# One layer of a hybrid decoder on one core: a block of weights multiplied in two products instead of three in three parts of the program

## The chip, the core and the metric

The kernel runs on one core of a Trainium2 chip. The metric is the device time of one execution in microseconds; three executions of the kernel before took 1103.18, 1103.72 and 1104.4 us, with a median of 1103.72 us.

## What is computed

The input x has 256 tokens of 2048 features, in float32, and there is one layer. The reference, cut to what matters:

```python
h = rmsnorm(x, attn_norm_g)
z = h @ w_in                                    # pool | q | k | v | indexer
y_pool = pool_mixer(u_pool, pool_w, pool_scale) # 4 groups, windows 2, 4, 8, 16
y_attn = dsa_attention(q, k, v, q_idx, k_idx, w_idx)
x = x + jnp.concatenate([y_pool, y_attn], axis=-1) @ w_out
up = rmsnorm(x, ffn_norm_g) @ w_up              # then a causal convolution of width 3
out = x + (silu(gate) * val) @ w_down
```

## The kernel before

**Exact splits.** Every float32 weight is split on the chip into a high part `whi` (ScalarE, L103) and a low part `wlo` (VectorE, L104), and so is every activation: `xhl` is the normalized x, `yhl` the mixers' output, `ghl` the gated feed-forward activation, each with a high and a low part of 256 tokens beside each other. A product of a weight block (128 x 128) and 256 tokens is the sum of three: high weight by high tokens, high weight by low tokens, low weight by high tokens.

**Two ways to form it with features on partitions.** `mm_feat` (L209 to 212) multiplies the high weight by both token parts in one instruction of 512 columns (L211), whose second 256 columns go to the second half of the PSUM bank, and the low weight by the high tokens in one of 256 columns (L212). Whoever reads the result must add the two halves. `mm_feat1` (L214 to 218) makes three products of 256 columns (L216, L217, L218) that all add up in the first half, so that there is nothing to add at the end. Each product loads its weight block first, so L216 and L217 load the same one twice. Before the change `mm_feat` serves w_up and the first 14 of the 16 output tiles of w_down; `mm_feat1` serves the pool columns of w_in (`pool_chunk`, L231), w_out (`mm_o`, L266), the last two tiles of w_down (t = 14 and 15, L316) and the small mixing matrices of the pool groups (`pool_mix`, L571). The other columns of w_in are formed with tokens on partitions (`mm_tok`, L205 to 207, products of 320 to 512 columns).

**Pieces.** The weights arrive as a stream of 384 pieces of up to 1024 columns (8 blocks each for the parts above). At step i the main loop asks for a load, splits piece i+2 (`prep`), calls the side work listed for step i (the `at(...)` table) and issues the products of piece i. `whi` and `wlo` have four buffers each. A scheduler then sets the final order on each engine.

**Accumulators.** `Acc` takes a [128, 2, 512] buffer, of which there are two, or for the last two w_down tiles a single bank. Readers are `pool_u` (L519, one multiplication by the norm, L522), `x1_out` (L580, adds the residual, L583, then splits the new x and sums its squares), `up_out` (L610), `down_out` (L636) and `down_out1` (L643, adds the residual and stores one tile, L646 and L647).

**The pool chain.** For each of four groups n: pool_u, then pool_win (sliding sums L533, difference L537, edges L540 and L542, split into `dhl` L544 and L545), then pool_mix (products `pm`, results into `yhl`, L573 and L574), all as side work between the pieces. The last group's columns are the last of w_in, and w_out follows directly; its first pair of tiles is ordered so that the rows of the last group come last.

Of the kernel before, what the change touches and what calls it, by code (L numbers as in the profile page):

```python
# [15 lines left out]
P = 128  # L16
# [11 lines left out]

# columns of the packed parameters
C_AG, C_FG, C_PS, C_QG, C_KG, C_IC, C_CW, C_CB = 0, 16, 32, 40, 41, 42, 58, 58 + 3 * 2 * NF  # L30
C_N = C_CB + 2 * NF

# the indexer's columns: heads (with the key and the head weights in the first chunk)
IHEADS = (5, 6, 5)
IWIDTH = (5 * 64 + 80, 6 * 64, 5 * 64)
# pool groups, the widest window first
GROUPS = (3, 2, 1, 0)
# the columns of w_in: indexer, keys, queries, values, pool groups
ORDER = ("i0", "i1", "i2", "k0", "k1", "u0", "q0", "q1", "u1", "v0", "u2", "v1", "u3")
# [4 lines left out]
def hybrid_kernel(ctx, tc, xT, par, wI0, wI1, wI2, wA, wU, wP, wO, wUp, wDn, out):  # L44
# [12 lines left out]

# [1 line left out]
    warm = cp.tile([P, 512], BF16, name="warm")  # L59
# [8 lines left out]
    nc.gpsimd.memset(ones, 1.0)  # L68
    # loads the table of functions
    tab = cp.tile([P, 1], F32, name="tab")  # L70
# [3 lines left out]

# [1 line left out]
    class Unit:  # L76
        """Columns of weights that are loaded together."""

# [12 lines left out]
    class Piece:  # L91
        """Columns a .. b of a unit, split together, and the products that use them."""

# [21 lines left out]

# [1 line left out]
    def split_x(k, src, gains, on_act):  # L117
# [16 lines left out]

# [1 line left out]
    def rsqrt_cols(pool, src, n, mul, name):  # L136
# [6 lines left out]
    class TokenNorm:  # L143
        """From a [P, S] sum of squares over features: r by token, as columns and along rows."""

# [27 lines left out]
    def squares(q):  # L173
        # not ahead of the first pieces
        act, dve = pieces[7].issued
        with tc.issue_after(act), tc.issue_after(dve):
            nc.scalar.activation(sqz[:, 0], xf[:, 4 * q:4 * q + 4], AF.Square)
            nc.vector.tensor_reduce(sqz[:, 1, q], sqz[:, 0].rearrange("p k t -> p t k"), axis=AX.X, op=ALU.add)  # L178
# [3 lines left out]

# [1 line left out]
    class Acc:  # L184
        """Accumulators [P, 2, 512] or [P, 512], taken when the first product is traced."""

# [10 lines left out]
    def mm_tok(acc, piece, ks, width):  # L197
        """tokens on partitions: acc[:, th, :width] += x[:, k].T @ w[k]."""
        pt = acc.get()
        for i, k in enumerate(ks):  # L200
            wh, wl = piece.get(i * width, width)
            for th in range(2):
                t = slice(th * P, (th + 1) * P)
                o = pt[:, th, :width]
                nc.tensor.matmul(o, xhl[:, k, 0, t], wh, start=(k == 0), stop=False)  # L205
                nc.tensor.matmul(o, xhl[:, k, 0, t], wl, start=False, stop=False)  # L206
                nc.tensor.matmul(o, xhl[:, k, 1, t], wh, start=False, stop=(k == KT - 1))  # L207

    def mm_feat(o, wh, wl, rhs, first, last):  # L209
        """features on partitions: o[:, 0:256] += w.T @ hi, + wl.T @ hi; o[:, 256:512] += wh.T @ lo."""  # L210
        nc.tensor.matmul(o, wh, rhs.rearrange("p a t -> p (a t)"), start=first, stop=False)  # L211
        nc.tensor.matmul(o[:, 0:S], wl, rhs[:, 0], start=False, stop=last)  # L212

    def mm_feat1(o, wh, wl, rhs, first, last):  # L214
        """The same, all in o[:, 0:256]."""
        nc.tensor.matmul(o[:, 0:S], wh, rhs[:, 0], start=first, stop=False)  # L216
        nc.tensor.matmul(o[:, 0:S], wh, rhs[:, 1], start=False, stop=False)  # L217
        nc.tensor.matmul(o[:, 0:S], wl, rhs[:, 0], start=False, stop=last)  # L218

    def tok_chunk(srcs, width, cuts=()):  # L220
        """16 k-tiles of `width` columns, in units of 4 and pieces of 2 k-tiles."""
        acc = Acc()
        for q in range(4):
            u = Unit(srcs[q], 4 * width, cuts[q] if q < len(cuts) else None)
            for h in range(2):
                def mm(p, k0=4 * q + 2 * h):
                    mm_tok(acc, p, (k0, k0 + 1), width)
                pieces.append(Piece(u, 2 * h * width, (2 * h + 2) * width, mm))
        return acc

    # ================= the stream of pieces =================  # L231
    def pool_chunk(n):
        acc = Acc()
        for j in range(2):
            u = Unit(wU[2 * n + j], D)
            for h in range(2):
                def mm(p, j=j, h=h):
                    pt = acc.get()
                    for i in range(8):
                        k = 8 * h + i  # L240
                        mm_feat1(pt[:, j], *p.get(i * P, P), xhl[:, k], k == 0, k == KT - 1)
                pieces.append(Piece(u, h * 1024, (h + 1) * 1024, mm))
# [16 lines left out]

    # rows of w_out: heads 0 .. 3, the first pool groups, heads 4 .. 7, the last pool group  # L260
    yhl = zc.tile([P, KT, 2, S], F32R, name="yhl")
# [4 lines left out]
    def mm_o(jp, j, ks, p, base):  # L266
        pt = oa[jp].get()
        for k in ks:
            mm_feat1(pt[:, j], *p.get((k - base) * P, P), yhl[:, k], k == 0, k == KT - 1)

# [35 lines left out]
    for i in range(16 * NF // 8):  # L306
# [3 lines left out]
        def mm(p, i=i):  # L310
            for n in range(8):
# [3 lines left out]
                else:  # L315
                    mm_feat1(da[t - 7].get(), *p.get(n * P, P), ghl[:, k], k == 0, k == NF - 1)  # L316
        o = (i % 2) * 1024
        pieces.append(Piece(u, o, o + 1024, mm))

    # ================= indexer =================  # L320
    qiT = [zc.tile([P, 8, S], F32R, name=f"qiT{c}", tag="big", bufs=2) for c in range(2)]
# [43 lines left out]
    def tr_iq(h0):  # L365
        """Heads h0 and h0 + 1: [hi; lo] on partitions."""
        tp = ps_s.tile([P, 512], F32, name="tp", tag="ss")
# [39 lines left out]

    # ================= attention =================
    gqk = zc.tile([P, 1], F32, name="gqk")
# [101 lines left out]

    # ================= pool channels: features on partitions =================
    pw_ = {}
# [4 lines left out]
    def pool_u(n):  # L518
        pt = ua[n].get()  # L519
        ub = wide("ub")  # L520
        nc.gpsimd.memset(ub[:, :, 0:16], 0.0)
        nc.vector.tensor_tensor(ub[:, :, 16:], pt[:, :, 0:S], r1.b2(), op=ALU.mult)  # L522
        pw_[n] = ub
# [52 lines left out]

    # ================= x1, its norm =================
    sq1 = cp.tile([P, 2, S], F32, name="sq1")

    def x1_out(jp):  # L580
        pt = oa[jp].get()
        x1 = xf[:, 2 * jp:2 * jp + 2]
        nc.vector.tensor_tensor(x1, pt[:, :, 0:S], x1, op=ALU.add)  # L583
        for j in range(2):
# [10 lines left out]

    # ================= ConvFFN =================
    fw = {}
# [45 lines left out]
    def down_out1(jp, j):  # L643
        pt = da[jp + j].get()
        t = fw["fp"].tile([P, 2, S], F32, name="ft", tag="ft", bufs=2)
        nc.vector.tensor_tensor(t[:, j], pt[:, 0:S], xf[:, 2 * jp + j], op=ALU.add)  # L646
        nc.scalar.dma_start(out[:, 2 * jp + j], t[:, j])  # L647

    # ================= what else happens at each piece =================
    at(9, nc.sync.dma_start, pr, par)  # L650
# [58 lines left out]

    # ================= the kernel =================  # L710
    def load(n):
# [90 lines left out]
```

## Time and profile before

| what | value |
|---|---|
| three executions | 1103.18, 1103.72, 1104.4 us |
| profiled execution, first to last instruction (span) | 1102.1 us |
| its own time with what lies around the span | not listed; the median of the runs is 1.6 us above the span |
| TensorE busy | 1092.7 us, 99% of the span, 6620 products |
| VectorE, ScalarE busy | 734.4 us (67%), 570.0 us (52%) |
| products of 256 columns in threes, with x, y, g | 3 x 128, 3 x 256, 3 x 88 |
| products of 512 and 256 in pairs | 2 x 1408, 2 x 616 |

PE is TensorE, PEld its weight loads, DVE VectorE, ACT ScalarE, POOL GpSimd, SP the engine that issues most DMAs. A product's shown duration holds its way through the array, and neighbours overlap; what it costs in a dense stream is the distance from its start to the next start.

### The profile page before, as it was taken

How to read it: one execution, taken by the hardware profiler on the slowest of the kernel's cores; microseconds unless marked ns; L12 is line 12 of the kernel's file. 1: busy time of each engine (PE TensorE's matmuls, PEld its weight loads, DVE VectorE, ACT ScalarE, POOL GpSimd, SP SyncE). 2: the span in 40 equal slices, each digit the busy share in tenths (PEclk: the TensorE clock that was granted, in tenths of full speed). 3: DMA queues.
4: the chain of work that ended last, by engine and by line, in shares of the span. 5: the costliest groups of instructions: out<-in, count | busy, mean ns of one | idle time of the engine just before them, and what ended most of it. 6: DMA issues, size and time to landing. Idle time of an engine off the chain costs nothing.

```text
span 1102.1 us, 16427 instructions
## 1 busy us (share of the span) xinstructions
PE 1092.7 (99%) x6620; PEld 974.2 (88%) x6620; DVE 734.4 (67%) x1034; ACT 570.0 (52%) x792; POOL 13.7 (1%) x25
## 2 busy tenths in 40 slices
PE   8999999999999999999999999999999999999998
PEld 6998989889999988888888888888888888888898
DVE  7767867665556677777877787878777544444442
ACT  6555456654444555555555555555555433344441
POOL 0001000000000000000000000000000000000000
PEclk9999999999999999999999999999999999999999
DMA  7554554444555555555555555555555555555552
GB/s 261 165 179 163 191 202 156 163 162 161 181 191 174 175 192 187 191 191 191 191 192 191 191 191 191 192 191 191 190 192 188 188 198 200 197 199 196 198 197 76
DMA packets 31755, 204.30 MB, mean 185 GB/s; under 512 B 3648, under 2 KB 4288, under 8 KB 8640
## 3 DMA queue, kind: packets, MB, share of 16 engines
q1 hardware_dynamic: 30240, 201.16, 53.4%
q10 hardware_dynamic: 1440, 2.11, 0.5%
q8 instruction: 52, 0.85, 0.3%
q14 instruction: 23, 0.19, 0.0%
HBM read 201.15 MB, written 2.10 MB: 184 GB/s over the span
## 4 chain that ended last, share of the span: by engine, by line
PE 96%; DVE 1%; DMA 1%; issue 1%; ACT 0%; SPq 0%; ACTq 0%; DVEq 0%
PE mm L211 43%; PE mm L212 21%; PE mm L218 5%; PE mm L217 5%; PE mm L216 5%; PE mm L206 5%; PE mm L205 5%; PE mm L207 5%; DMA raw<-in_wI_dram 1%; DVE wlo L104 1%; PE sp L381 1%; PE sp L467 0%; DVE sqz L178 0%; PE tp L455 0%; PE tp L371 0%
## 5 line engine op out<-in xcount | busy, mean ns | idle before, releaser
L104 DVE TENSOR_TENSOR wlo<-raw,whi 128x1024 fp32r<-128x1024 f32 (+4 forms) x385 | 462.1, 1202 | 297.4 <-ACT whi L103 297.3
L103 ACT ACTIVATE whi<-raw 128x1024 fp32r<-128x1024 f32 (+4 forms) x385 | 399.9, 1041 | 428.8 <-PE mm L211 260.4
L211 PE MATMUL mm<-xhl,whi 128*128 128x512 f32 x1408 | 488.5, 394 | 0.0
L212 PE MATMUL mm<-xhl,wlo 128*128 128x256 f32 x1408 | 390.1, 277 | 0.0
L211 PEld LDWEIGHTS mm<-xhl,whi 128*128 128x128 f32 x1408 | 264.0, 188 | 61.3
L212 PEld LDWEIGHTS mm<-xhl,wlo 128*128 128x128 f32 x1408 | 264.2, 188 | 0.0
L211 PE MATMUL mm<-ghl,whi 128*128 128x512 f32 x616 | 213.6, 394 | 0.0
L212 PE MATMUL mm<-ghl,wlo 128*128 128x256 f32 x616 | 170.6, 277 | 0.0
L211 PEld LDWEIGHTS mm<-ghl,whi 128*128 128x128 f32 x616 | 115.5, 188 | 26.9
L212 PEld LDWEIGHTS mm<-ghl,wlo 128*128 128x128 f32 x616 | 115.6, 188 | 0.0
L205 PE MATMUL mm<-whi,xhl 128*128 128x512 f32 (+3 forms) x288 | 108.6, 377 | 2.3 <-ACT xhl L120 0.8
L206 PE MATMUL mm<-wlo,xhl 128*128 128x512 f32 (+3 forms) x288 | 107.0, 371 | 2.5 <-DVE wlo L104 2.4
L207 PE MATMUL mm<-whi,xhl 128*128 128x512 f32 (+3 forms) x288 | 106.8, 371 | 0.0
L216 PE MATMUL mm<-yhl,whi 128*128 128x256 f32 x256 | 72.6, 284 | 0.0
L218 PE MATMUL mm<-yhl,wlo 128*128 128x256 f32 x256 | 72.4, 283 | 0.0
L217 PE MATMUL mm<-yhl,whi 128*128 128x256 f32 x256 | 72.4, 283 | 0.0
L206 PEld LDWEIGHTS mm<-wlo,xhl 128*128 128x128 f32 x288 | 54.1, 188 | 10.7 <-DVE wlo L104 4.0
L205 PEld LDWEIGHTS mm<-whi,xhl 128*128 128x128 f32 x288 | 54.1, 188 | 10.5 <-ACT whi L103 1.8
L207 PEld LDWEIGHTS mm<-whi,xhl 128*128 128x128 f32 x288 | 54.1, 188 | 8.3 <-DVE xhl L123 0.5
L217 PEld LDWEIGHTS mm<-yhl,whi 128*128 128x128 f32 x256 | 49.1, 192 | 0.0
L216 PEld LDWEIGHTS mm<-yhl,whi 128*128 128x128 f32 x256 | 49.1, 192 | 0.0
L218 PEld LDWEIGHTS mm<-yhl,wlo 128*128 128x128 f32 x256 | 49.1, 192 | 0.0
(155 smaller groups left out, 928.9 us busy)
## 6 DMA issues: line engine op xcount, KB each, us to landing
raw<-in_wUp_dram SPq DMA_DIRECT2D x88, 1024.0 KB, 4.8
raw<-in_wDn_dram SPq DMA_DIRECT2D x44, 1024.0 KB, 4.8
raw<-in_wA_dram SPq DMA_DIRECT2D x24, 1024.0 KB, 4.8
raw<-in_wO_dram SPq DMA_DIRECT2D x16, 1024.0 KB, 4.8
raw<-in_wU_dram SPq DMA_DIRECT2D x8, 1024.0 KB, 4.8
raw<-in_wI_dram SPq DMA_DIRECT2D x4, 768.0 KB, 4.2
raw<-in_wI_dram SPq DMA_DIRECT2D x7, 400.0 KB, 5.2
raw<-in_wI_dram SPq DMA_DIRECT2D x4, 640.0 KB, 4.1
```

The source lines that it names most:

```text
L103: i1 = nc.scalar.activation(hi, raw, AF.Copy)
L104: i2 = nc.vector.tensor_tensor(self.lo[:, c:c + n], raw, hi.bitcast(F32), op=ALU.subtract)
L205: nc.tensor.matmul(o, xhl[:, k, 0, t], wh, start=(k == 0), stop=False)
L206: nc.tensor.matmul(o, xhl[:, k, 0, t], wl, start=False, stop=False)
L207: nc.tensor.matmul(o, xhl[:, k, 1, t], wh, start=False, stop=(k == KT - 1))
L211: nc.tensor.matmul(o, wh, rhs.rearrange("p a t -> p (a t)"), start=first, stop=False)
L212: nc.tensor.matmul(o[:, 0:S], wl, rhs[:, 0], start=False, stop=last)
L216: nc.tensor.matmul(o[:, 0:S], wh, rhs[:, 0], start=first, stop=False)
L217: nc.tensor.matmul(o[:, 0:S], wh, rhs[:, 1], start=False, stop=False)
L218: nc.tensor.matmul(o[:, 0:S], wl, rhs[:, 0], start=False, stop=last)
L381: nc.tensor.matmul(sp[:, a:b], q, kiT[:, e, 0:b - a], start=(e == 0), stop=(e == 1))
```

## The change

In three places `mm_feat` takes the place of `mm_feat1`, and the readers of these accumulators add the second half. Comments and docstrings are also dropped, and line numbers after them move. The core:

```diff
 def pool_chunk(n):
...
-                        mm_feat1(pt[:, j], *p.get(i * P, P), xhl[:, k], k == 0, k == KT - 1)
+                        mm_feat(pt[:, j], *p.get(i * P, P), xhl[:, k], k == 0, k == KT - 1)
 def mm_o(jp, j, ks, p, base):
...
-            mm_feat1(pt[:, j], *p.get((k - base) * P, P), yhl[:, k], k == 0, k == KT - 1)
+            mm_feat(pt[:, j], *p.get((k - base) * P, P), yhl[:, k], k == 0, k == KT - 1)
                 if t < 14:
                     mm_feat(da[t // 2].get()[:, t % 2], *p.get(n * P, P), ghl[:, k], k == 0, k == NF - 1)
                 else:
-                    mm_feat1(da[t - 7].get(), *p.get(n * P, P), ghl[:, k], k == 0, k == NF - 1)
+                    mm = mm_feat if t == 14 or k < NF - 6 else mm_feat1
+                    mm(da[t - 7].get(), *p.get(n * P, P), ghl[:, k], k == 0, k == NF - 1)
 def pool_u(n):
...
-        nc.vector.tensor_tensor(ub[:, :, 16:], pt[:, :, 0:S], r1.b2(), op=ALU.mult)
+        uv = ub[:, :, 16:]
+        nc.scalar.activation(uv, pt[:, :, S:2 * S], AF.Copy)
+        nc.vector.tensor_tensor(uv, pt[:, :, 0:S], uv, op=ALU.add)
+        nc.vector.tensor_tensor(uv, uv, r1.b2(), op=ALU.mult)
 def x1_out(jp):
...
+        nc.vector.tensor_tensor(x1, pt[:, :, S:2 * S], x1, op=ALU.add)
         nc.vector.tensor_tensor(x1, pt[:, :, 0:S], x1, op=ALU.add)
 def down_out1(jp, j):
...
-        nc.vector.tensor_tensor(t[:, j], pt[:, 0:S], xf[:, 2 * jp + j], op=ALU.add)
+        nc.vector.tensor_tensor(t[:, j], pt[:, S:2 * S], xf[:, 2 * jp + j], op=ALU.add)
+        nc.vector.tensor_tensor(t[:, j], pt[:, 0:S], t[:, j], op=ALU.add)
```

For the very last tile (t = 15) the last 6 of its 44 blocks stay in threes, so the second half of its bank gets its last columns six blocks before the end.

The scheduler's order at the places that matter. In the rows below the names in brackets are semaphores that an instruction waits for, by the engine or DMA queue that raises them.

VectorE at the end of the program, from the residual of tile 14 on (`ft` is the tile that is stored). Before:

```order
L646 TENSOR_TENSOR ft<-mm_9786,xf 128x256 [waits DMAHW1_49,PE_49]
L104 TENSOR_TENSOR wlo<-raw,whi 128x1024 [waits DVE_49,DMAHW1_49,PE_49,Activation_49]
L104 TENSOR_TENSOR wlo<-raw,whi 128x1024 [waits DVE_49,PE_49,Activation_49]
L646 TENSOR_TENSOR ft<-mm_9943,xf 128x256 [waits DMAHW7_49,PE_49]
L797 UNCONDITIONAL_BRANCH
```

and now:

```order
L652 TENSOR_TENSOR ft<-mm_9418,xf 128x256 [waits DMAHW1_49,PE_49]
L653 TENSOR_TENSOR ft<-mm_9418,ft 128x256 [waits DVE_49]
L104 TENSOR_TENSOR wlo<-raw,whi 128x1024 [waits DMAHW1_49,PE_49,Activation_49]
L104 TENSOR_TENSOR wlo<-raw,whi 128x1024 [waits PE_49,Activation_49]
L652 TENSOR_TENSOR ft<-mm_9531,xf 128x256 [waits DMAHW7_49,PE_49]
L653 TENSOR_TENSOR ft<-mm_9531,ft 128x256 [waits DVE_49]
L804 UNCONDITIONAL_BRANCH
```

Each residual is now two additions; the first of a pair waits for PE, the second for VectorE alone.

VectorE at the join of w_in and w_out, for the last pool group (`ub` the group's columns, `win` sums, `d` difference, `dhl` its split; `yhl<-op` belongs to attention heads). Before:

```order
L522 TENSOR_TENSOR ub<-mm,r1b 128x2x256 [waits PE_49]
L533 TENSOR_TENSOR win<-ub 128x2x271 [waits DVE_49,Pool_49]
L510 TENSOR_TENSOR yhl<-op,yhl 128x256 [waits Activation_49]
L537 SCALAR_TENSOR_TENSOR d<-win,ub 128x2x256 [waits DVE_49]
L540 TENSOR_TENSOR dfix<-win,pr 128x2
L104 TENSOR_TENSOR wlo<-raw,whi 128x1024
L542 TENSOR_TENSOR d<-dfix,ub 128x2 [waits DVE_49]
L545 TENSOR_TENSOR dhl<-d,dhl 128x2x256 [waits Activation_49]
```

and now:

```order
L104 TENSOR_TENSOR wlo<-raw,whi 128x1024 [waits PE_49,Activation_49]
L512 TENSOR_TENSOR yhl<-op,yhl 128x256 [waits Activation_49]
L526 TENSOR_TENSOR ub<-mm,ub 128x2x256 [waits Activation_49]
L527 TENSOR_TENSOR ub<-ub,r1b 128x2x256 [waits DVE_49]
L538 TENSOR_TENSOR win<-ub 128x2x271 [waits DVE_49,Pool_49]
L512 TENSOR_TENSOR yhl<-op,yhl 128x256 [waits Activation_49]
L542 SCALAR_TENSOR_TENSOR d<-win,ub 128x2x256 [waits DVE_49]
L545 TENSOR_TENSOR dfix<-win,pr 128x2
L104 TENSOR_TENSOR wlo<-raw,whi 128x1024 [waits DMAHW1_49,Activation_49]
L547 TENSOR_TENSOR d<-dfix,ub 128x2 [waits DVE_49]
L104 TENSOR_TENSOR wlo<-raw,whi 128x1024 [waits PE_49,Activation_49]
L550 TENSOR_TENSOR dhl<-d,dhl 128x2x256 [waits Activation_49]
```

A weight split and a head's result now stand ahead of `ub`, and one more weight split stands ahead of the low half of `dhl`. ScalarE, which makes the high half of `dhl`, before:

```order
L509 ACTIVATE yhl<-op 128x256 [waits PE_49]
L544 ACTIVATE dhl<-d 128x2x256 [waits DVE_49]
L509 ACTIVATE yhl<-op 128x256 [waits PE_49]
L103 ACTIVATE whi<-raw 128x1024 [waits DMAHW1_49,Activation_49]
L103 ACTIVATE whi<-raw 128x1024 [waits PE_49,Activation_49]
L573 ACTIVATE yhl<-pm,pr 128x256 [waits PE_49] x2
```

and now:

```order
L511 ACTIVATE yhl<-op 128x256 [waits PE_49]
L525 ACTIVATE ub<-mm 128x2x256
L511 ACTIVATE yhl<-op 128x256 [waits PE_49]
L103 ACTIVATE whi<-raw 128x1024 [waits DMAHW1_49,DVE_49]
L103 ACTIVATE whi<-raw 128x1024 [waits DVE_49,PE_49]
L549 ACTIVATE dhl<-d 128x2x256 [waits DVE_49]
L578 ACTIVATE yhl<-pm,pr 128x256 [waits PE_49] x2
```

The two weight splits that followed `dhl` now precede it, and the second of them waits for PE. On PE the products `pm` that read `dhl` stood after two whole pieces of w_out; now they are mixed into the third:

```order
L211 MATMUL mm<-yhl,whi 128x512 [waits DVE_49]
L216 MATMUL pm<-dhl,pwh 128x256 [waits PE_49,Activation_49]
L216 MATMUL pm<-dhl,pwh 128x256 [waits PE_49]
L212 MATMUL mm<-yhl,wlo 128x256
L211 MATMUL mm<-yhl,whi 128x512 [waits DVE_49]
L212 MATMUL mm<-yhl,wlo 128x256
L211 MATMUL mm<-yhl,whi 128x512
L212 MATMUL mm<-yhl,wlo 128x256
L211 MATMUL mm<-yhl,whi 128x512
L217 MATMUL pm<-dhl,pwh 128x256 [waits DVE_49]
L218 MATMUL pm<-dhl,pwl 128x256
```

PE's list is 6079 rows long now, where it was 6545.

## Rows read from the trace of the kernel before

**Rows 1.** The page: engines, the granted TensorE clock in 40 slices, the chain's shares.

```profile
PE 1092.7 (99%) x6620; PEld 974.2 (88%) x6620; DVE 734.4 (67%) x1034; ACT 570.0 (52%) x792; POOL 13.7 (1%) x25
...
PEclk9999999999999999999999999999999999999999
...
PE 96%; DVE 1%; DMA 1%; issue 1%; ACT 0%; SPq 0%; ACTq 0%; DVEq 0%
```

**Rows 2.** Busy time by stretch: PE, PEld, DVE, ACT, POOL, granted clock, DMA share, GB/s.

```profile
100.00:150.00 50.00, 50.00 (x273) 43.58 (x272) 41.16 (x90) 21.73 (x26) 4.89 (x5) 1.00 0.54 184
...
300.00:350.00 50.00, 50.00 (x420) 50.00 (x418) 29.64 (x34) 23.32 (x29) 0.00 (x0) 1.00 0.53 182
```

**Rows 3.** Lines L211 and L216, w_up and w_down: duration ns, first and last start us.

```profile
L211 PE MATMUL mm<-xhl,whi x1408: 391/395/476, 364.3 to 853.0; 128*128 128x512 f32 x176
...
L211 PE MATMUL mm<-ghl,whi x616: 392/394/396, 853.4 to 1066.6; 128*128 128x512 f32 x154
...
L216 PE MATMUL mm<-ghl,whi x88: 280/283/284, 1066.9 to 1098.2; 128*128 128x256 f32 x88
```

**Rows 4.** Groups of instructions by line and shape: the threes with y and with x.

```profile
L216 PE MATMUL mm<-yhl,whi 128*128 128x256 f32 x256 | 72.6, 284 | 0.0
...
L216 PE MATMUL mm<-xhl,whi 128*128 128x256 f32 x128 | 37.3, 291 | 0.0
```

**Rows 5.** PE in order of time (start, us): w_in of 320 and 512 columns, w_out.

```profile
49.94 0.31 PE L207 MATMUL mm<-whi,xhl 128*128 128x320 f32 x1
...
50.82 0.31 PE L207 MATMUL mm<-whi,xhl 128*128 128x320 f32 x1
...
129.65 0.39 PE L205 MATMUL mm<-whi,xhl 128*128 128x512 f32 x1
...
131.47 0.39 PE L207 MATMUL mm<-whi,xhl 128*128 128x512 f32 x1
...
300.20 0.28 PE L216 MATMUL mm<-yhl,whi 128*128 128x256 f32 x1
...
303.80 0.28 PE L216 MATMUL mm<-yhl,whi 128*128 128x256 f32 x1
```

**Rows 6.** The end in order of time: last product, residual, store.

```profile
1098.48 0.28 PE L218 MATMUL mm<-ghl,wlo 128*128 128x256 f32 x1
1098.80 0.42 DVE L646 TENSOR_TENSOR ft<-mm,xf 128x256 f32<-128x256 f32 x1 [9.26 <-PE mm L218]
1099.25 0.34 ACTq L647 DMA_DIRECT2D out_dram<-ft  x1
```

**Rows 7.** Groups by line and shape: readers of accumulators, 128 x 512.

```profile
L614 DVE TENSOR_TENSOR ft<-mm,ft 128x512 f32<-128x512 f32 x44 | 30.0, 683 | 0.0
L613 ACT ACTIVATE ft<-mm 128x512 f32<-128x512 f32 x44 | 25.4, 577 | 0.0
...
L583 DVE TENSOR_TENSOR xf<-mm,xf 128x512 f32<-128x512 f32 x8 | 5.5, 692 | 8.6 <-PE mm L218 8.6
```

**Rows 8.** The last pool group, DVE in order of time.

```profile
269.59 0.69 DVE L522 TENSOR_TENSOR ub<-mm,r1b 128x512 f32<-128x512 f32 x1 [0.86 <-PE mm L218]
270.39 0.72 DVE L533 TENSOR_TENSOR win<-ub 128x542 f32<-128x542 f32 x1
...
274.02 0.69 DVE L545 TENSOR_TENSOR dhl<-d,dhl 128x512 fp32r<-128x512 f32 x1 [0.70 <-ACT dhl L544]
```

**Rows 9.** The same stretch on ACT and PE.

```profile
273.36 0.63 ACT L544 ACTIVATE dhl<-d 128x512 fp32r<-128x512 f32 x1 [2.56 <-DVE d L542]
...
276.59 1.06 ACT L103 ACTIVATE whi<-raw 128x1024 fp32r<-128x1024 f32 x1 [1.38 <-PE mm L217]
...
276.45 0.28 PE L216 MATMUL pm<-dhl,pwh 128*128 128x256 f32 x1
```

**Rows 10.** A weight split early in the queries, and the piece that reads it.

```profile
135.59 1.23 DVE L104 TENSOR_TENSOR wlo<-raw,whi 128x1024 fp32r<-128x1024 f32 x1 [1.38 <-ACT whi L103]
...
138.49 0.39 PE L205 MATMUL mm<-whi,xhl 128*128 128x512 f32 x1
```

## The prediction

> **What bounds the kernel now.** The page comes first [rows 1]: TensorE is busy for 1092.7 of 1102.1 us and holds 96% of the chain that ends last, and the granted clock is full in all 40 slices. By stretch [rows 2] it is busy for all of 50 us in w_in and in w_out, at a granted clock of 1.00, which is the higher of its two levels, 2.4 GHz. VectorE, the next busiest, reaches 41.16 of 50 us between 100 and 150 us and 29.64 in w_out. So a nanosecond taken off the dense stream of products is a nanosecond off the end, as long as nothing that feeds the stream comes later than it does now.
>
> What a product costs is then read from starts, not from durations. w_down shows both ways with the same operands [rows 3]: 616 pairs with g, from the first start at 853.4 us to the last at 1066.6 us, are 213.2 us over 615 steps, 346.7 ns a block; 88 threes, from 1066.9 to 1098.2 us, are 31.3 us over 87 steps, 359.8 ns. w_up's pairs, from 364.3 to 853.0 us with a few other products between them, are 347.3 ns over 1407 steps. In w_out, 10 blocks in threes take 303.80 - 300.20 = 3.60 us, 360 ns a block [rows 5].
>
> Why a pair is cheaper can be read too. In w_in six steps of 320 columns take 50.82 - 49.94 = 0.88 us, 146.7 ns each, and eight of 512 columns take 131.47 - 129.65 = 1.82 us, 227.5 ns each [rows 5]. The line through both has 0.42 ns a column and some 12 ns that do not depend on columns. By it 256 columns cost 120 ns, as the threes do. A pair and a three have the same 768 columns; the three pays those 12 to 13 ns once more.
>
> The Trainium skill, "TensorE: Matmul & The Clock Gate", section "Back-to-back issue gap", speaks against this size: columns over 2.4 plus 2.5 ns for an isolated product at the full clock, so one product less would be worth 2.5 ns a block and 1.2 us over 466 blocks. The rows differ (13.1 ns between 359.8 and 346.7), and the measurement decides.
>
> **The change, part by part.**
>
> *Removed: one product a block.* The blocks in question are 128 with x, 256 with y [rows 4] and 88 with g [rows 3], of which the last 6 stay as they are: 128 + 256 + 82 = 466. PE's list is shorter by exactly that, 6545 - 6079. Each saves 13.1 ns by w_down and 13.3 by w_out's 360. I take 13.2: 466 x 13.2 = 6.15 us, with ends at 6.10 and 6.20.
>
> *Added: reading the second half.* `pool_u`, four times: a ScalarE copy out of PSUM like up_out's, 577 ns, and a VectorE addition like L614's, 683 ns [rows 7], before the multiplication that was there, 0.69 us [rows 8]. `x1_out`, eight times: one more addition like L583's, 692 ns [rows 7]. In w_out VectorE has 20 of 50 us idle [rows 2] and the accumulator is wanted again only after the other one's four pieces, 4 x 8 x 0.347 = 11.1 us; I cost the eight at nothing. If that cover were gone, they would be 8 x 0.69 = 5.5 us.
>
> *The first pool group.* Here VectorE is fullest. Its queue holds weight splits behind `pool_u`; the one at 135.59 us ends at 136.82 us, and the piece that reads it starts at 138.49 us, 1.67 us later [rows 10]. The change takes 32 x 13.2 ns = 0.42 us from this lead, because PE is through the pool columns sooner, and 0.69 us for the addition. 0.56 us are left, so nothing is lost; the 1.38 us that VectorE sits idle ahead of that split, waiting for ScalarE, absorb part of it. Bounds: 0 to 0.5 us. I take 0.
>
> *The last pool group.* Now the chain from the group's last product to `dhl` goes from 269.59 us to the end of its low half at 274.02 + 0.69 = 274.71 us [rows 8], and the products `pm` start at 276.45 us [rows 9]: 1.7 us to spare. Afterwards the copy and the addition come in, and so does the new order: ScalarE splits two weight pieces before it makes the high half, and the second waits for PE to finish the second piece of w_out, as the split at 276.59 us does now, 0.14 us after PE was through with that piece [rows 9]. Pieces are 8 x 0.347 = 2.77 us instead of 2.88, so that split starts at about 276.59 - 2 x 0.11 - 0.1 = 276.2 us on the old time scale, ends at 277.3, and the high half (0.63 us [rows 9]) at 277.8. The low half comes behind another VectorE split (1.2 us from 277.3) and takes 0.69: 279.1 us. PE gets to its first `pm` four blocks and one long product after the second piece, which ends at 276.45 - 0.23 - 0.1 = 276.1: 277.7 us. It needs the low half two `pm` and some three blocks on, at 279.0 us. So PE waits about 0.1 us at each, together 0.25 us. Bounds: 0, if each step is a little shorter; 0.9, if PE stands at the low half through the whole addition and a hand-over. A quarter of a microsecond is what the rows give, and I take it.
>
> *The end.* The final residual now has two additions. One could lie under the last six blocks, whose columns of the second half are finished 6 x 0.36 = 2.2 us before. But in the order on VectorE the second addition, which reads the half that the very last product writes, waits for VectorE only. So the wait for the last product is already in the first, and both stand behind it. Now one addition of 0.42 us starts at 1098.80 and the store is issued at 1099.25 us [rows 6]. A second adds 0.42 us and a hand-over, which between dependent instructions there lies at 0.1 us or less (0.69 us from 269.59 to 270.28, next start 270.39 [rows 8]): 0.42 to 0.53 us. I take 0.47.
>
> *Sum.* -6.15 + 0.25 + 0.47 = -5.43 us. The profiled execution's span of 1102.1 us becomes 1096.7; its own time is not listed, the median of the runs is 1.6 us above the span, and I keep that distance: 1103.72 - 5.43 = **1098.3 us**.
>
> **The rivals.**
>
> *The join stalls for a piece.* `dhl` now stands behind a split whose weights come by DMA and whose buffer PE must free. If one of these is late by a piece, PE waits for 2.8 us at `pm`: 1098.3 + 2.8 = 1101.1 us. For it: the spare time of 1.7 us is gone by my own reckoning. Against it: the splits there run well ahead of the products. Chance 0.05.
>
> *Only w_down gains.* The fixed cost of a product is measured with g in both ways and with tokens in the rows of w_in, but x and y in the two ways only once each. If in w_in and w_out it were hidden behind the stream of weight loads, 82 x 13.2 ns = 1.1 us would be left, and after 0.47 at the end 1103.1 us: no change. The section of the Trainium skill named above gives about the same size by another way. Against it: w_out's threes show the same 360 ns as w_down's. Chance 0.04.
>
> *Slower: VectorE sets the pace.* The additions stand in VectorE's queue ahead of weight splits. If a split's lead is smaller than what the addition takes (0.69 us, and 0.42 more in the pool columns), PE waits for all of it, each time. Wholly uncovered, 12 additions are 8.3 us and 4 copies 2.3; with 0.47 at the end and 6.15 gained it comes to 1103.72 + 4.9 = 1108.6 us. It decides where a lead falls below 1.1 us. Speaking for it is only the stretch with 41.16 busy of 50; speaking against it are a lead of 1.67 us there [rows 10] and VectorE's 29.64 of 50 in w_out [rows 2]. Chance 0.03.
>
> That the change does not do what it says is no rival: the order shows the products gone.
>
> **How the numbers follow.** The forecast has a chance of 0.88. Its range takes the ends of the terms: -6.20 + 0 + 0.42 gives 1097.9, -6.10 + 0.9 + 0.5 + 0.53 gives 1099.6; the runs of the kernel before lie 0.5 us below and 0.7 us above their median, which I add by half: 1097.6 to 1099.9 us. That leaves out 0.12 and needs nothing more. About 0.2%, 2.2 us, is what a measurement of this kernel can tell from no change; the forecast (5.4 us faster) and the first rival (2.6) lie beyond it: faster 0.93, within 0.04, slower 0.03.
>
> **What would show it.** In the profile after: starts 347 ns apart by block in the pool columns and w_out; w_up's first product at 359.5 us (now 364.3 [rows 3], less 384 x 13.2 ns = 5.07, plus 0.25 at the join); w_down's last tile 0.5 us shorter; PE idle, if anywhere, only at `pm` of the last group; two additions after the last product and a store 0.47 us later behind it. It is wrong if blocks in w_out stay at 360 ns, if PE shows waits for `wlo` behind `pool_u`, or if the first addition at the end starts before the last product.

## The result, and the profile after

The changed kernel takes **1112.1 us** (median of 20 runs), the kernel before 1103.6 us (20 runs beside it): a ratio of 1.0074 with a 95% interval from 1.0063 to 1.0085. It is 8.6 us slower where 5.4 us less was forecast. Nineteen of the 20 executions lie between 1111.7 and 1113.9 us, and one took 1100.94 us. Both kinds show the granted clock at full, so the clock is not what divides them. There is a trace of each kind: the profiled execution of this measurement is the one at 1100.94 us, and the first experiment below, the same kernel again (median 1111.9 us), has a profiled execution of the usual kind. "The usual trace" below means that one.

The page of the usual trace, the lines that answer to [rows 1]:

```profile
span 1110.0 us, 15516 instructions
...
PE 1101.8 (99%) x6154; PEld 955.8 (86%) x6154; DVE 742.9 (67%) x1048; ACT 571.9 (52%) x796; POOL 13.7 (1%) x25
...
PEclk9999999999999999999999999999999999999999
...
PE 96%; DMA 2%; DVE 1%; issue 1%; ACT 0%; SPq 0%; ACTq 0%; DVEq 0%
```

and of the execution at 1100.94 us:

```profile
span 1099.2 us, 15516 instructions
...
PE 1089.4 (99%) x6154; PEld 949.4 (86%) x6154; DVE 741.8 (67%) x1048; ACT 572.5 (52%) x796; POOL 13.8 (1%) x25
```

Fewer products (6154 records, 6620 before), and more time in them. No engine has become the bound: TensorE holds 96% of the chain as before, VectorE is at 67% as before. So TensorE does not wait more; it goes slower. The stretches answer to [rows 2] (PE, PEld, DVE, ACT, POOL busy, clock, DMA share, GB/s). The usual trace in w_out, w_up and w_down:

```profile
300.00:350.00 50.00, 50.00 (x290) 43.70 (x289) 33.56 (x41) 24.78 (x31) 0.00 (x0) 1.00 0.56 190
400.00:800.00 400.00, 400.00 (x2267) 346.86 (x2266) 301.40 (x426) 223.82 (x319) 0.00 (x0) 1.00 0.55 186
900.00:1050.00 150.00, 150.00 (x851) 130.07 (x850) 71.40 (x63) 58.77 (x59) 0.00 (x0) 1.00 0.58 195
```

and the execution at 1100.94 us:

```profile
300.00:350.00 50.00, 50.00 (x285) 43.35 (x284) 32.12 (x38) 24.37 (x30) 0.00 (x0) 1.00 0.54 184
400.00:800.00 400.00, 400.00 (x2309) 349.81 (x2308) 306.28 (x434) 228.91 (x326) 0.00 (x0) 1.00 0.56 190
900.00:1050.00 150.00, 150.00 (x867) 131.20 (x866) 72.87 (x65) 59.75 (x59) 0.00 (x0) 1.00 0.58 199
```

PE is busy for all of each stretch at full clock, but gets through different numbers of the same products: 2267 or 2309 in the 400 us of w_up, 290 or 285 in 50 us of w_out. Two products (a pair, one of 512 and one of 256 columns) are a block: 400 / 1133.5 = 353 ns in the one case and 400 / 1154.5 = 346.5 ns in the other; in w_out it is the other way round. The pairs by line (duration ns, first and last start) give it more finely. Usual trace:

```profile
L211 PE MATMUL mm<-yhl,whi x256: 391/395/477, 267.8 to 358.7; 128*128 128x512 f32 x128
...
L211 PE MATMUL mm<-xhl,whi x1373: 395/398/404, 372.1 to 856.9; 128*128 128x512 f32 x197
...
L211 PE MATMUL mm<-ghl,whi x698: 394/398/404, 857.2 to 1103.5; 128*128 128x512 f32 x175
```

Execution at 1100.94 us:

```profile
L211 PE MATMUL mm<-yhl,whi x256: 393/398/476, 269.2 to 361.7; 128*128 128x512 f32 x128
...
L211 PE MATMUL mm<-xhl,whi x1380: 391/392/474, 372.3 to 850.8; 128*128 128x512 f32 x198
...
L211 PE MATMUL mm<-ghl,whi x698: 392/394/395, 851.2 to 1092.8; 128*128 128x512 f32 x175
```

w_down's 698 pairs are 246.3 us over 697 steps, **353.4 ns a block**, in the usual trace, and 241.6 us, **346.6 ns**, in the other. Before, they took 346.7 [rows 3]. The usual trace also has w_up at 484.8 us over 1372 steps, 353.4 ns. From 372.1 us to the end about 2070 blocks cost 6.7 ns more each: 13.9 us.

The balance of the usual trace against the one before: w_up's first product at 359.1 us against 364.3 [rows 3], 5.2 us earlier; from there to the last product 1105.89 - 359.1 = 746.8 us against 1098.48 - 364.3 = 734.2 [rows 6], 12.6 us more; and 0.5 us more behind it. That sums to 7.9 us, the difference of the spans. 1.1 of the 5.2 us lie ahead of the first changed product (115.0 us against 116.1; the other execution has 116.4), so they are the scatter of the start and not the change's. The change gained 4.1 us up to w_up, and lost three times that in two stages of which it touches only the last two tiles.

### The profile page after: what moved, and what is told of

Its sections match the earlier page's. It is cut to its first block, busy times and chain, and to the rows that moved or that the text cites. A ratio compares the mean times of both kernels' runs of the same rounds, so it can differ in the third digit from the quotient of the medians.

```text
span 1099.2 us, 15516 instructions
## 1 busy us (share of the span) xinstructions
PE 1089.4 (99%) x6154; PEld 949.4 (86%) x6154; DVE 741.8 (67%) x1048; ACT 572.5 (52%) x796; POOL 13.8 (1%) x25
## 3 DMA queue, kind: packets, MB, share of 16 engines
q10 hardware_dynamic: 1440, 2.11, 0.5%
## 4 chain that ended last, share of the span: by engine, by line
PE 95%; DMA 2%; DVE 1%; issue 1%; ACT 0%; SPq 0%; ACTq 0%; DVEq 0%
PE mm L211 53%; PE mm L212 26%; PE mm L205 4%; PE mm L207 4%; PE mm L206 4%; DMA raw<-in_wI_dram 2%; DVE wlo L104 1%; PE sp L383 1%; PE sp L469 0%; DVE sqz L178 0%; PE tp L457 0%; PE tp L373 0%; PE op L509 0%; PE tp L497 0%; ACT whi L103 0%
## 5 line engine op out<-in xcount | busy, mean ns | idle before, releaser
L211 PE MATMUL mm<-xhl,whi 128*128 128x512 f32 x1536 | 535.0, 395 | 0.0
L212 PE MATMUL mm<-xhl,wlo 128*128 128x256 f32 x1536 | 425.9, 277 | 0.0
L211 PEld LDWEIGHTS mm<-xhl,whi 128*128 128x128 f32 x1536 | 288.1, 188 | 66.7
L212 PEld LDWEIGHTS mm<-xhl,wlo 128*128 128x128 f32 x1536 | 288.6, 188 | 0.2
L211 PE MATMUL mm<-ghl,whi 128*128 128x512 f32 x698 | 242.0, 394 | 0.0
L212 PE MATMUL mm<-ghl,wlo 128*128 128x256 f32 x698 | 193.3, 277 | 0.0
L211 PEld LDWEIGHTS mm<-ghl,whi 128*128 128x128 f32 x698 | 130.9, 188 | 30.4
L211 PE MATMUL mm<-yhl,whi 128*128 128x512 f32 x256 | 90.8, 399 | 0.0
L211 PEld LDWEIGHTS mm<-yhl,whi 128*128 128x128 f32 x256 | 48.1, 188 | 11.8
L638 ACT ACTIVATE ghl<-fc 128x256 fp32r<-128x256 f32 x44 | 18.4, 417 | 57.9 <-DVE fc L637 57.9
L629 ACT ACTIVATE fc<-up,pr 128x256 f32<-128x256 f32 x88 | 47.5, 587 | 0.1
```

The source lines that it names most:

```text
L629: nc.scalar.activation(c[:, j], u[:, j, 2:], AF.Identity, bias=pr[:, C_CB + n:C_CB + n + 1], scale=cw[2])
L638: nc.scalar.activation(ghl[:, f, 0], c[:, 0], AF.Copy)
```

## The experiments

Two theories stood at first. **A**: the stream of pairs settles into one of several rhythms (a rhythm is the repeating pattern of the distances between the products' starts), which holds until something else is put between the products; the change only alters how w_up is entered. **B**: what the change added (readers, places in memory) slows the last stages. A third, **C**, came up behind the first runs: the rhythm is drawn by chance in each execution.

**The parts, one at a time.** The first run is the changed kernel again. In the other three, two of its three edits are taken back (`mm_feat1` in place of `mm_feat`, and the additions taken out with it); w_out alone differs from the kernel before by

```diff
 mm_o
-            mm_feat1(pt[:, j], *p.get((k - base) * P, P), yhl[:, k], k == 0, k == KT - 1)
+            mm_feat(pt[:, j], *p.get((k - base) * P, P), yhl[:, k], k == 0, k == KT - 1)
 x1_out
+        nc.vector.tensor_tensor(x1, pt[:, :, S:2 * S], x1, op=ALU.add)
```

The changed kernel again:

> The changed kernel again, for a profile of an execution near 1112 us. Theory A (pattern): a stream of pairs settles into one of several repeating patterns of start times; 346.7 ns a block in w_up of the one profile so far, 353.3 ns in its pool columns and w_out, and which pattern w_up and w_down get is decided where they are entered. An execution of 1112 us then has blocks of about 352 to 354 ns over most of w_up's and w_down's 2106 pairs (2106 x 5 to 6.6 ns = 11 to 14 us), no longer starts-to-start gap than now at piece borders, and TensorE without idle time. Theory B (readers): the added copies and additions make PE wait for weights or accumulators in these executions; blocks stay at 347 ns, and about 11 us of gaps show in w_in and w_out, before w_up starts.

Pool columns alone:

> Only the pool columns of w_in in pairs, with their readers; w_out and the last tiles in threes as before. Own saving if blocks take 353.3 ns: 128 x 6.7 = 0.9 us. Theory A: 1102.5 to 1103 us unless the order of products later in w_in shifts what w_up is entered with; w_up is entered out of w_out's threes exactly as before, so its blocks stay at 347 ns. Theory B: the pool chain is the one that stalls (copy, two additions), so that most of the 11 us show here: 1110 us or more.

w_out alone:

> Only w_out in pairs, with x1_out's second addition. Own saving if blocks take 353.3 ns: 256 x 6.7 = 1.7 us. Theory A: the entry of w_up is now out of pairs, as in the changed kernel, so this one shows two kinds of time, about 1102 us where w_up has 347 ns and about 1112 us where it has not. Theory B: VectorE is half idle in w_out, nothing waits, 1102 us in every execution.

The last two w_down tiles alone:

> Only the last two w_down tiles in pairs, with the second addition of each residual. Nothing before 1066 us differs. Theory A: the stream just runs on in the pattern it has, 82 x 13.2 = 1.1 us less, and 0.4 to 0.5 us more at the end for the addition behind the last product: 1102.9 to 1103.1 us. Theory B: the same number.

Measured: again 1111.88 us (ratio 1.0079, 1.0064 to 1.0094); pool columns 1102.66 (0.9993, 0.9984 to 1.0003); w_out 1100.36 (0.9970, 0.9960 to 0.9981); w_down 1103.00 (0.9996, 0.9987 to 1.0005), beside 1103.52 us. No part alone is slow, and the parts add up to 4.5 us less, not 8.4 more. In all three traces w_up behind its first 16 blocks, and w_down, run at 347 ns a block. That fits A. One expectation was a miss: w_out alone showed no second kind of time in eight runs, and it took 1100.4 us where about 1102 was expected, because its w_out runs at 347 ns and not at 353.

**Taking the loss away, and making it without the change.** Reading the starts of the traces side by side, the rhythm changes within w_up and w_down only where float32 products of the norm stand between two pieces of w_up: the sums at L152 (one column) and the broadcast at L163 (128 columns). (In w_out it changes at the last pool group's products `pm`.) So such products were put in a second time, to be read by nobody. G0 is the step of w_up's first piece, O0 that of w_out's. Into the changed kernel:

```diff
+    def kick():
+        pc = ps_s.tile([P, 512], F32, name="pk", tag="ss")
+        for th in range(2):
+            nc.tensor.matmul(pc[:, th:th + 1], sq1[:, 0, th * P:(th + 1) * P], ones[:, 0:1], start=True, stop=True)
     at(G0 + 4, r2.rows)
+    at(G0 + 6, kick)
```

> The changed kernel with two more float32 products of one column (two in name, four matmul records, like the ones at L152 that sum the squares) put between two w_up pieces, two pieces after the norm's last products. They compute nothing that is read. Theory A (the stream of pairs keeps the rhythm in which it was last entered, 347 or 353 ns a block): in the traces so far a stream at 353 ns went over to 347 ns after products of this kind, and a stream at 347 ns stayed there. So from there to the end 347 ns a block; beside the changed kernel's usual 1111.9 us about 2050 blocks x 6.6 ns = 13.5 us less and 0.4 us more for the products: 1098.8 us (1098.0 to 1099.8). Theory B (something that the change put on the engines or in memory slows the last two stages, whatever the entry): no gain, 1112.3 us. Theory C (the rhythm is drawn by chance in each execution, rarely a good one): again mostly 1112 us, once in some twenty runs 1101 us.

Measured 1098.84 us (0.9959, 0.9944 to 0.9974). In its trace the pairs between L163 and the insertion, and those behind it:

```profile
L211 PE MATMUL mm<-xhl,whi x16: 393/398/478, 371.4 to 376.8; 128*128 128x512 f32 x16
...
L211 PE MATMUL mm<-xhl,whi x1339: 392/395/395, 384.9 to 848.7; 128*128 128x512 f32 x192
L211 PE MATMUL mm<-ghl,whi x698: 392/394/395, 849.1 to 1090.7; 128*128 128x512 f32 x175
```

The first row has a median duration of 398, the mark of the slower rhythm above; behind the insertion it is 463.8 / 1338 = 346.6 ns a block, and it stays so to the end. Four useless matmuls bought 13 us.

Into the kernel **before**, in which all parts of the change are absent:

```diff
+    def kick():
+        pb = ps_s.tile([P, 512], F32, name="pk", tag="ss")
+        for th in range(2):
+            nc.tensor.matmul(pb[:, th * P:(th + 1) * P], ones, r2.dg[:, th], start=True, stop=True)
+    at(G0 + 6, kick)
```

> The kernel before, with no part of the change, and the two products of 128 columns of L163 (the norm's broadcast) done a second time into a tile that nobody reads, two pieces later in w_up. Theory A: in the changed kernel's 1110.0 us trace a stream at 347 ns went over to 353 ns after products of this kind, and the kernel before runs at 347 ns at that place; so 353 ns a block in the 1352 blocks left of w_up and the 616 pairs of w_down: 1968 x 6.6 ns = 13.0 us and 0.4 us for the products more, 1117 us (1115.5 to 1118) without anything of the change. Theory B: 0.4 us more, 1103.9 us. Theory C: some runs at one and some at the other.

Measured 1117.03 us (1.0125, 1.0110 to 1.0140). Its pairs behind the insertion:

```profile
L211 PE MATMUL mm<-xhl,whi x1353: 395/398/403, 384.9 to 862.6; 128*128 128x512 f32 x194
L211 PE MATMUL mm<-ghl,whi x616: 395/398/403, 862.9 to 1080.2; 128*128 128x512 f32 x154
```

477.7 / 1352 = 353.3 ns: the same loss, without the change. And with the products of one column two pieces later in that same kernel (`at(G0 + 6, kick)`, `at(G0 + 8, kick_c)`):

> The kernel before with the second set of broadcast products (which alone made it 1117.0 us) and, two pieces later, the four products of one column that brought the changed kernel back to 347 ns. Theory A (a rhythm holds until the next cut, and the cut sets the next one): 353 ns for 16 blocks only, so 1103.2 + 0.4 + 0.4 + 16 x 6.6 ns = 1104.1 us (1103.6 to 1104.8). If the loss of the second set has another cause (its tile, its place in memory): 1117.4 us.

Measured 1104.38 us (1.0008, 0.9999 to 1.0018). The loss is made and taken back by insertions alone. Theory B is out: neither the readers nor anything else of the change is needed for the loss, and with all of it in place the loss can be removed. So is C as the main cause, for each of these three kernels has one kind of time in every run. Chance has a smaller part: behind `pm`, w_out runs at 353 ns in three traces of kernels with the pool columns and w_out both in pairs (the executions at 1100.94, 1099.69 and 1100.09 us) and at 347 ns in the other six, and traces of one and the same kernel stand on both sides.

**The better parts together, and a second insertion.** w_out and w_down in pairs, pool columns in threes:

> The change in w_out and w_down, the pool columns left in threes. If the parts simply add: w_out alone gave 3.2 us and w_down 0.5 us, so 1099.9 us (1099.3 to 1100.4), under theory A too if w_up is entered as with w_out alone, which has the same instructions up to w_down. Theory A allows nothing else here: w_down's last tiles come after the whole stream. Theory B, with the pool columns as the part at fault, says the same; with w_down's last tiles at fault only together with w_out, 1112 us.

Measured 1098.89 us (0.9962, 0.9948 to 0.9976). It is 0.4 us below the expected range: 4.3 us less than the kernel before beside it, where the parts alone sum to 3.7. Where these 0.6 us lie is not shown; the first pool product starts anywhere from 115.0 to 116.4 us in the traces here, so the scatter of the start alone is as large. The changed kernel with an insertion in w_out as well (`at(O0 + 8, kick_o)`, the same four products with `ident` for the sum of squares):

> The changed kernel with the four float32 matmuls of one column put twice: at w_out's ninth piece and two pieces after the norm's last products in w_up. Theory A: w_out leaves 353 ns, if it is there, at the ninth piece (24 pieces x 8 x 6.6 ns = 1.3 us), for 0.4 us, and w_up and w_down run at 347 ns: as with the one insertion or up to 0.9 us less, 1097.9 to 1099.2 us. Theory B: 1112.7 us. Theory C: mostly 1112 us.

Measured 1099.76 us (0.9967, 0.9956 to 0.9979), 0.6 us outside the expected range. In its trace w_out already runs at 347 ns when the insertion comes, so it had nothing to win; the span is 0.4 us longer than with one insertion (1097.6 against 1097.2). The other half of the 0.9 us between the two medians was not traced to a place. With w_out and w_down in pairs and three pool groups too (`mm_feat if n < 3 else mm_feat1` in `pool_chunk`, the additions in `pool_u` likewise):

> w_out and w_down in pairs as in the run that had these two alone (1098.9 us), and pool groups 0 to 2 in pairs too; the last pool group, whose products are the last ones ahead of w_out, stays in threes, so w_out is entered as there. Theory A: w_out and w_up as there, and three quarters of what the pool columns gave alone (0.75 us): 1098.3 us (1097.7 to 1098.7). If instead the entry into w_up is decided by the start-up of the whole stream, some 1112 us are possible.

Measured **1098.05 us** (0.9951, 0.9938 to 0.9963). That beats both kernels, and is the lowest median of all, though not clear of 1098.6 and 1098.9 us in what follows.

**Where the rhythm is cut.** Four useless products are not a fix to keep. In the usual trace w_up reaches L163 in a rhythm that repeats every two blocks, so it has two halves at which it can be cut. Moving L163's products by one block adds no instruction:

```diff
             def mm(p, f=f, j=j, h=h):
                 pt = ga_[f].get()
                 for i in range(8):
+                    if (f, j, h, i) == (0, 1, 1, 7):
+                        r2.rows()
                     k = 8 * h + i
-    at(G0 + 4, r2.rows)
```

One block earlier:

> The changed kernel with the norm's last products (L163) one block earlier in w_up, behind an odd number of pairs since the products before them instead of an even one; no instruction is added. In the changed kernel's usual run this place is reached at 347 ns in the rhythm that repeats every two blocks, and left at 353 ns. Theory A1 (what counts is at which half of that rhythm it is cut): the other half may be left at 347 ns; then about 2056 blocks x 6.6 ns = 13.6 us less, 1098.3 us (1097.8 to 1099). Theory A2 (only the kind of the products and the rhythm before them count): 353 ns as before, 1111.9 us (1111.3 to 1112.5).

Two blocks earlier (`(0, 1, 1, 6)`), the same half as in the change:

> The same with the products two blocks earlier, so that the rhythm of two blocks is cut at the same half as in the changed kernel. Theories A1 and A2 both: 353 ns to the end, 1111.9 us (1111.3 to 1112.5). If it is 1098 us, the place counts in some other way than by the half of the rhythm.

Measured: one block 1098.85 us (0.9959, 0.9945 to 0.9972), two blocks 1112.57 us (1.0071, 1.0050 to 1.0092; 0.07 us above the expected range) with one run of ten at 1100.09. So it is not the place inside a piece that helps, for both stand inside one. The profiled execution of either (1099.69 and 1100.09 us) ran w_out at 353 ns, like the one at 1100.94 us above, and entered w_up in another rhythm; so these traces did not show the cut itself. For two blocks the cut is argued from the times alone: there is no trace of one of its runs near 1112 us. The kernel with one block twice more was to catch the cut:

> The kernel with the norm's last products one block earlier once more, for a trace in which w_out runs at 347 ns a block. Theory A1: in such a trace the products cut the rhythm of two blocks at its other half, and the blocks behind them take 347 ns, not 353; 1098.3 us (1098 to 1099.8). Theory A2: in such a trace w_up and w_down run at 353 ns, 1112 us.

> The same as odd_again, in case that one's trace shows w_out at 353 ns again: 1098.3 us (1098 to 1099.8), and 347 ns a block behind the products.

and three blocks earlier (`(0, 1, 1, 5)`):

> The changed kernel with the norm's last products three blocks earlier in w_up, an odd number as with one block, at another place. Theory A1: as with one block earlier, 1098.5 us (1098.0 to 1099.8), each of the runs. If only the one place is left well: mostly 1112 us.

Measured 1097.97 and 1097.85 us (one run each, 0.03 and 0.15 us below the expected range), and 1098.61 us (0.9954, 0.9938 to 0.9971). All three traces run w_out at 347 ns and go on at 347 ns behind L163. The cut in order of time on PE (start, us), first the usual trace of the change:

```profile
369.91 0.39 PE L211 MATMUL mm<-xhl,whi 128*128 128x512 f32 x1
370.14 0.27 PE L212 MATMUL mm<-xhl,wlo 128*128 128x256 f32 x1
370.25 0.40 PE L211 MATMUL mm<-xhl,whi 128*128 128x512 f32 x1
370.48 0.28 PE L212 MATMUL mm<-xhl,wlo 128*128 128x256 f32 x1
370.60 0.61 PE L163 MATMUL pb<-dg,ones 128*128 128x128 f32 x4
370.96 0.48 PE L211 MATMUL mm<-xhl,whi 128*128 128x512 f32 x1
...
371.40 0.39 PE L211 MATMUL mm<-xhl,whi 128*128 128x512 f32 x1
...
371.75 0.40 PE L211 MATMUL mm<-xhl,whi 128*128 128x512 f32 x1
...
372.11 0.40 PE L211 MATMUL mm<-xhl,whi 128*128 128x512 f32 x1
...
372.45 0.40 PE L211 MATMUL mm<-xhl,whi 128*128 128x512 f32 x1
...
373.51 0.40 PE L211 MATMUL mm<-xhl,whi 128*128 128x512 f32 x1
```

and the kernel with the products one block earlier:

```profile
369.69 0.40 PE L211 MATMUL mm<-xhl,whi 128*128 128x512 f32 x1
...
370.04 0.39 PE L211 MATMUL mm<-xhl,whi 128*128 128x512 f32 x1
370.27 0.28 PE L212 MATMUL mm<-xhl,wlo 128*128 128x256 f32 x1
370.38 0.60 PE L163 MATMUL pb<-dg,ones 128*128 128x128 f32 x4
370.75 0.47 PE L211 MATMUL mm<-xhl,whi 128*128 128x512 f32 x1
...
371.17 0.40 PE L211 MATMUL mm<-xhl,whi 128*128 128x512 f32 x1
...
371.52 0.39 PE L211 MATMUL mm<-xhl,whi 128*128 128x512 f32 x1
...
371.87 0.40 PE L211 MATMUL mm<-xhl,whi 128*128 128x512 f32 x1
...
372.21 0.39 PE L211 MATMUL mm<-xhl,whi 128*128 128x512 f32 x1
...
373.25 0.40 PE L211 MATMUL mm<-xhl,whi 128*128 128x512 f32 x1
```

Up to the cut the long products take 0.39 and 0.40 us in turn. The last one ahead of it takes 0.40 us in the first (370.25) and 0.39 in the second (370.04): the two halves. Behind it the six blocks from 371.40 to 373.51 us take 2.11 us in the first, 352 ns each, and the six from 371.17 to 373.25 take 2.08 in the second, 347 ns each. In ns, the last long product ahead of the broadcast products takes 395 in all five traces that go on at 353 (the usual one, the two with one-column products put in behind it, and the kernel before with the broadcast put in a second time, without and with one-column products behind it) and 392 in all three that reach the cut in the rhythm of two blocks and go on at 347 (one block earlier twice, three blocks earlier). Read more finely, the starts within a block (long product to short one, short one to the next) show three rhythms: every block 230 + 117 ns; two blocks in turn, 231 + 112 and 233 + 117; three blocks in turn, 232 + 118, 241 + 120 and 236 + 113. The first two have a mean of 347 ns, the third of 353.

What each kernel's trace shows, in ns a block (a: all blocks alike, b: two in turn; threes: w_out as before the change):

| kernel | w_out behind `pm` | w_up to L152 | L152 to L163 | behind L163 | us |
|---|---|---|---|---|---|
| before | threes, 360 | 353 | 347 a | 347 b | 1103.5 |
| pool or w_down alone | threes, 360 | 353 | 347 a | 347 b | 1102.7, 1103.0 |
| change, usual | 347 b | 347 b | 347 b | 353 | 1111.9 |
| change, the one run | 353 | 353 | 347 a | 347 b | 1100.9 |
| w_out alone; w_out and w_down; pool 0 to 2 too | 347 a | 347 a | 347 a | 347 b | 1100.4; 1098.9; 1098.1 |
| L163 one block earlier again (twice); three blocks earlier | 347 b | 347 b | 347 b | 347 b | 1098.0, 1097.9; 1098.6 |
| L163 one or two blocks earlier, the profiled executions | 353 | 353 | 347 a | 347 b | 1099.7, 1100.1 |

In every trace here one-column products led from 353 to 347 and left either rhythm of 347 as it was; the broadcast products led from a to b, and from b to 353 or to b, by the half at which they cut it.

## Why the prediction was wrong

*The step that failed* is the one on what a product costs: 347 ns was taken for the price of a pair, when it is what a pair costs in two of three rhythms. The forecast summed 466 blocks x 13.2 ns and put the effect on the 2,024 pairs which the change does not touch [rows 3] at nothing, without a reason. It is the largest term: in the usual trace these pairs run at 353.4 ns from L163 to the end, 13.9 us with the 82 new ones, because the change alters the rhythm in which w_up reaches L163 and so the one in which it leaves it. None of the three signs of being wrong that the prediction named came, and none of its rivals was this one. The trace of before held a warning that the prediction did not have. Its w_up starts, up to L152, with

```profile
L211 PE MATMUL mm<-xhl,whi x16: 395/398/403, 364.3 to 369.6; 128*128 128x512 f32 x16
```

5.3 us over 15 steps, 353 ns, with products of the same shape and tiles that run at 347 ns ten microseconds later. The mean over w_up (347.3 ns) hides it: the prediction put what it has over 346.7 down to "a few other products", and most of these 0.9 us is indeed theirs, while 15 steps at 353 add 0.1.

*With the rhythm held, the sum was near.* The changed kernel with L163 one block earlier has every edit of the change and no instruction more or fewer: 1098.0, 1097.9 and (median of 4) 1098.9 us, where 1098.3 was forecast in a range from 1097.6 to 1099.9. The four run from 1098.1 to 1099.7 us; the profiled one is the slowest and ran w_out at 353 ns, the two single ones ran it at 347. Some luck is in the two single ones: in the first, the first changed product starts at 115.1 us, 1.0 ahead of before's. From there its span is 5.8 - 1.0 = 4.8 us shorter, where 5.4 was forecast; the pool columns are what is short. Term by term:

*w_out.* Forecast 256 x 13.2 = 3.38 us. w_out alone goes from its first product at 269.6 to w_up's at 360.6 us, 91.0 us against 364.3 - 270.0 = 94.3 before: 3.3 us. The rival "only w_down gains" would have had nothing here. The Trainium skill, "TensorE: Matmul & The Clock Gate", section "Back-to-back issue gap", has 2.5 ns beyond the columns for an isolated product at the full clock, and says itself that this formula is not that of a stream with weight loads; taken all the same, an estimate by it is 256 x 2.5 = 0.6 us, and the trace does not agree with that.

*Pool columns.* Forecast 128 x 13.2 = 1.69 us. From the first pool product to w_out's first it is 268.9 - 116.1 = 152.8 us with the pool columns alone in pairs, against 270.0 - 116.1 = 153.9 before: 1.1 us. The prediction had 347 ns there. In the traces of the change the first and the last group run at 353 ns, and some 64 blocks x 6.6 ns = 0.4 us is most of what is missing; the rest was not traced to a place.

*w_down's last tiles and the end.* Forecast 82 x 13.2 = 1.08 us less and 0.47 us more; w_down alone gave 1103.52 - 1103.00 = 0.5 us. The end of the usual trace:

```profile
1105.89 0.28 PE L218 MATMUL mm<-ghl,wlo 128*128 128x256 f32 x1
1106.21 0.42 DVE L652 TENSOR_TENSOR ft<-mm,xf 128x256 f32<-128x256 f32 x1 [9.09 <-PE mm L218]
1106.67 0.42 DVE L653 TENSOR_TENSOR ft<-mm,ft 128x256 f32<-128x256 f32 x1
1107.12 0.34 ACTq L654 DMA_DIRECT2D out_dram<-ft  x1
```

The first addition waits for the very last product, as the order said, and from that product's start to the store it is 1.23 us against 0.77 [rows 6]: 0.46.

*The joins.* The last pool group's chain in the usual trace, on PE, ScalarE and VectorE:

```profile
275.57 0.40 PE L211 MATMUL mm<-yhl,whi 128*128 128x512 f32 x1
275.88 0.51 PE L216 MATMUL pm<-dhl,pwh 128*128 128x256 f32 x2
276.23 0.28 PE L212 MATMUL mm<-yhl,wlo 128*128 128x256 f32 x1
...
275.21 0.62 ACT L549 ACTIVATE dhl<-d 128x512 fp32r<-128x512 f32 x1
...
276.48 0.69 DVE L550 TENSOR_TENSOR dhl<-d,dhl 128x512 fp32r<-128x512 f32 x1
...
277.28 0.33 PE L217 MATMUL pm<-dhl,pwh 128*128 128x256 f32 x1
277.44 0.28 PE L218 MATMUL pm<-dhl,pwl 128*128 128x256 f32 x1
```

The high half ends at 275.83 us. Its first product starts 0.31 us after the long product ahead of it (275.57 and 275.88) instead of 0.23, and the two products that read it take 0.35 us to the next start instead of 0.24: 0.19 us. The low half ends at 277.17 us, and the product that reads it takes 0.16 us to the next start instead of 0.12: 0.04. Together they are some 0.23 us, where 0.25 was taken: the term was right. The rival "the join stalls for a piece" did not happen.

*VectorE* was the rival for a slower kernel, with 1108.6 us. The time came out beyond it, but not by its way: VectorE's share is unchanged, and the lost time lies in stages where the change gives it nothing to do until the last tiles. x1_out's eight additions and the first pool group cost nothing that a trace shows, as forecast.

**What stays open.** What in the hardware keeps such a rhythm was not measured; the runs show only when it changes. In the usual trace and in the execution at 1100.94 us the steps between the starts of the last pool group's `pm` products differ by 6 ns at most, and yet behind them w_out goes on at 347 ns in the one and at 353 in the other; why is not known. It decides which kind of time an execution of the change has: entered at 353 ns, w_up is at 347 a behind L152 and at 347 b behind L163; entered at 347 b, it is cut at the bad half. A residual whose first addition runs under the last six blocks, for the 0.4 us at the end, wasn't tried.

## What to carry to other kernels

A gain counted as "so many instructions times so many ns" holds only while the rest of a dense stream keeps its pace: after any edit ahead of a long uniform stretch, compare the number of products in a fixed window of a stage that the edit does not touch. If it moved with TensorE busy and the clock unchanged, look at the starts around whatever interrupts the stream, and move the interruption by one block before giving the edit up. And when a trace shows the same instruction at two paces, explain that before pricing with their mean.

## What the runs showed of the hardware that was not expected

A stream of fp32r pairs (512 and 256 columns) on one TensorE at full granted clock has at least three stable patterns of starts, two with a mean of 347 ns a block and one of 353 (1.9% apart). A pattern held for over 700 us and some 2,000 blocks, across the change from w_up to w_down and across every buffer turn. Four small float32 matmuls cost 0.4 us (spans 1097.2 and 1097.6 us with one and two sets) and can switch it for 13 us, either way (1111.9 to 1098.8 us, 1103.2 to 1117.0). For those of 128 columns their place, to the block, decides (1098.9 us one block earlier, 1112.6 two); those of one column were not moved.
